# 192 bytes a partition set aside between a kernel's split weights and its operand tiles

## The chip, the core and the metric

The kernel runs on one core of a Trainium2 chip. A core has five engines that run beside each other: PE (TensorE, matmuls; its weight loads are listed apart as PEld), DVE (VectorE), ACT (ScalarE), POOL (GpSimd) and SP (SyncE, which here issues DMAs). They share one on-chip memory of 128 partitions; a tile takes so many bytes in each partition, and an address below is the byte within the partition. The metric is the device time of one execution in microseconds (us), lower is better.

## What is computed

Two layers of a decoder trunk over 256 tokens and 1,024 features, all in float32. Each layer is a mixer and a feed-forward part (FFN), both with adaptive modulation (`w_ada`). Cut to the matrix products that matter here:

```
h    = rms_norm(x) * (1 + sc1) + sh1
proj = h @ w_in[l]                       # 1024 x 10840: q, k, v, index, z, xbc, dt, gates
o_attn = dsa_attention(q, k, v, iq, ik, iw) @ w_attn_o[l]
o_ssm  = gated_norm(ssd_scan(conv(xbc), dt), z) @ w_ssm_o[l]
x    = x + g1 * ((sigmoid(ga) * o_attn + sigmoid(gm) * o_ssm) @ w_out[l])
h    = rms_norm(x) * (1 + sc2) + sh2
val, gate = split(causal_dwconv(h @ w_up[l]))      # 1024 x 5632
x    = x + g2 * ((silu(gate) * val) @ w_down[l])   # 2816 x 1024
```

## The kernel before

**The products.** A float32 product is made of three matmuls of type `float32r`. Each operand is split into a high and a low part, and high x high, high x low and low x high are added up in PSUM. In one matmul one operand is *stationary* (loaded into PE's array first, 128 x 128; this is the PEld row of the profile) and the other is *moving* (streamed past it, 256 or 512 columns). The weights arrive in units of at most 4 x 128 rows by 512 columns (1 MB): `load` (L755) issues the DMA into a tile `st`, and `split_now` (L776) makes `wh` on ACT (a copy with rounding) and `wl = st - wh` on DVE, three buffers each. Activations are split in the same way into pairs of 256 columns.

**Two shapes.** `run_fm` (L798) keeps the weights stationary and moves the activations, 256 columns a matmul; per row block `k` and output block `m` it does

```
mm(o, u["hi"][:, k, ms], ah, kk == 0 and first[m], False)
mm(o, u["hi"][:, k, ms], al, False, False)
mm(o, u["lo"][:, k, ms], ah, False, last)
```

`run_tm` (L847, for q, k, v and the index) does it the other way round: the activations are stationary and 512 columns of the weights move. The trace names a matmul by its operands, the moving one first: `bk<-h,wh` is a moving `h` against a stationary `wh`, `bk<-wh,h` is the `run_tm` form. `bk` is the PSUM bank.

**The moving tiles.** `h` (`h_tile`, L461, pool `hp`, 16 buffers) holds the normalised input of a mixer or an FFN, and later the merged mixer output. `u` (`u_tile`, L456, pool `up`, 39 buffers) holds attention output, scan output and the FFN's activation. The last pairs of an FFN's activation go to `gate` (in the trace `t`, the tag `t2` of pool `wk`) and to `xdt0`/`xdt1`; the last pairs of the scan output go to `xdt` too. The first weight chunk after a norm (`Link`, L546) starts before the norm is known: it uses raw products in tiles `dec` (in the trace `p`, tag `p6` of `wk`) and `cbm`, with 2 columns more, 258 in all.

**Where tiles lie.** A pool's tiles stand one behind the other, in the order in which the pools were opened and the tags first used:

```
cst = ctx.enter_context(tc.tile_pool(name="cst", bufs=1))
wpool = ctx.enter_context(tc.tile_pool(name="wpool", bufs=3))
hp = ctx.enter_context(tc.tile_pool(name="hp", bufs=16))
wk = ctx.enter_context(tc.tile_pool(name="wk", bufs=2))
```

(L441 to L444); `up` is opened later and lies last, up to byte 228,896. `wpool` begins at 26,656, which is 52 x 512 + 32, and all its tiles, those of `hp` and those of `up` are multiples of 512 bytes long. So in the built program every `st`, `wh`, `wl`, `h` and `u` begins at 32 mod 512; so do their slices, which step by 512 bytes (a 128-column block) or 2,048 (a row block). The tiles of `wk` that take part in a product with `wh` and `wl` begin elsewhere because small tiles lie between them:

| moving tile | start mod 512 | minus start of `wh`, `wl` (32), mod 512 |
|---|---|---|
| `h`, `u`, `t` | 32 | 0 |
| `p` | 288 | 256 |
| `xdt`, `cbm` | 480 | 448 |

**What sets the order.** All instructions are recorded and then issued by a planner in the kernel (`commit`, L184; every instruction of the profile therefore has line L201), which fixes each engine's order from its own estimates of cost before anything runs. On the chip each engine works through its queue in that order and waits on semaphores.

**The FFN.** Its first product runs in 11 chunks of 96 matmuls (2 units, 4 output blocks, 4 row blocks each, 3 matmuls); the first chunk is a `Link`. Of each chunk ACT, DVE and POOL make a convolution of width 3 (`conv`, L1857), a tanh gate (`make_ev`, L1867) and the split of the activation (`hi_lo`, L1258), in between the splits of the next weights and the folding of `w_ada` (`adacc`).

Of the kernel before, what the change touches and what calls it, by code (L numbers as in the profile page):

```python
# [10 lines left out]
F32 = mybir.dt.float32  # L11
# [8 lines left out]
P = 128  # L20
# [26 lines left out]
def trunk(ctx, tc, x, c, positions, w_ada, b_ada, norm1_g, w_in, q_norm_g, k_norm_g, ssm_conv_w, ssm_conv_b,  # L47
# [393 lines left out]
    cst = ctx.enter_context(tc.tile_pool(name="cst", bufs=1))  # L441
    wpool = ctx.enter_context(tc.tile_pool(name="wpool", bufs=3))
    hp = ctx.enter_context(tc.tile_pool(name="hp", bufs=16))
    wk = ctx.enter_context(tc.tile_pool(name="wk", bufs=2))  # L444
    pj = ctx.enter_context(tc.tile_pool(name="pj", bufs=4, space=PSUM))
    sm = ctx.enter_context(tc.tile_pool(name="sm", bufs=4, space=PSUM))
# [1481 lines left out]
```

## Time and profile before

| | |
|---|---|
| median of 3 runs | 1256.91 us (1256.19 to 1258.14) |
| the profiled execution | 1256.64 us, of which its span (first to last instruction) is 1254.9 us |
| granted PE clock over the span | 0.998 |
| PE busy | 1229.9 us, 9833 matmuls |
| DVE, ACT, POOL busy | 989.0, 777.3, 478.4 us |
| read from HBM | 243.89 MB, 195 GB/s over the span |

How to read it: the profile is one execution, 0.27 us under the median. Matmuls are pipelined, so the duration of one (about 0.28 us) is latency, and the pace is read from the starts of neighbours. The time goes in this order: to 63 us the opening; 63 to 462 us the mixer of layer 0; 462 to 590 us the first product of its FFN and 590 to about 643 us its `w_down`; then the mixer of layer 1 to 1046 us, its FFN's first product to 1174 us, and `w_down` to the end.

### The profile page before, as it was taken

The page shows a single profiled execution, that of the slowest core. Times are in us where ns is not written, and L with a number is a line of the kernel's source. Part 1 is how long each engine was busy: PE and PEld are TensorE (multiplying, and loading weights), DVE is VectorE, ACT ScalarE, POOL GpSimd, SP SyncE. Part 2 cuts the span into 40 slices and gives each one's busy share as a digit, 9 for nine tenths or more (in the row PEclk, how much of TensorE's full clock was granted, in tenths as well). Part 3 has the DMA queues.
Part 4 walks back from the last instruction along what each step waited for, and adds up shares of the span by engine and source line. Part 5 has one row for each costly group of instructions (what it writes and reads, how often), then busy time and mean ns, then how long its engine had stood idle before and what let it go on. Part 6 is the DMA issues. An engine that isn't in the chain of part 4 may idle for free.

```text
span 1254.9 us, 24795 instructions
## 1 busy us (share of the span) xinstructions
PE 1229.9 (98%) x9833; PEld 1148.5 (92%) x9833; DVE 989.0 (79%) x1549; ACT 777.3 (62%) x1397; POOL 478.4 (38%) x503
## 2 busy tenths in 40 slices
PE   8999999999999999999999999999999999999998
PEld 7777889999999999999996878999999999999998
DVE  5599997877877789998677999887788667887752
ACT  4465767765774477776454476877478435877731
POOL 2162622342343226775121553414316222556500
PEclk9999999999999999999999999999999999999999
DMA  9854654555565747777847555444654665556551
GB/s 296 279 194 144 216 177 143 188 187 185 198 208 191 252 142 252 249 228 243 277 143 270 170 189 177 160 160 160 209 203 162 214 221 177 170 190 197 201 184 52
DMA packets 158665, 246.55 MB, mean 196 GB/s; under 512 B 11868, under 2 KB 66870, under 8 KB 158549
## 3 DMA queue, kind: packets, MB, share of 16 engines
q1 hardware_dynamic: 157989, 244.77, 58.6%
q8 instruction: 77, 1.26, 0.4%
q14 instruction: 39, 0.32, 0.1%
q0 software_dynamic: 288, 0.19, 0.1%
q10 hardware_dynamic: 272, 0.00, 0.0%
HBM read 243.89 MB, written 1.05 MB: 195 GB/s over the span
## 4 chain that ended last, share of the span: by engine, by line
PE 81%; DVE 10%; ACT 3%; POOL 2%; issue 2%; DMA 1%; SPq 0%; DVEq 0%; ACTq 0%; POOLq 0%
PE bk L201 81%; DVE wl L201 3%; POOL w L201 2%; DVE w L201 1%; ACT wh L201 1%; DVE t L201 1%; ACT w L201 1%; DMA ad<-in_w_ada_dram 1%; DVE mx L201 1%; DVE adacc L201 1%; DVE sp_p L201 1%; DVE p L201 1%; POOL rr L201 0%; DVE u L201 0%; DMA rows<-in_b_ada_dram 0%
## 5 line engine op out<-in xcount | busy, mean ns | idle before, releaser
L201 PE MATMUL bk<-h,wh 128*128 128x256 f32 x3296 | 611.9, 286 | 1.2 <-ACT h L201 1.1
L201 PEld LDWEIGHTS bk<-h,wh 128*128 128x128 f32 x3296 | 513.9, 192 | 11.2 <-issue 8.0
L201 DVE TENSOR_TENSOR wl<-st,wh 128x2048 fp32r<-128x2048 f32 (+1 forms) x200 | 438.7, 2199 | 90.4 <-ACT wh L201 89.8
L201 PE MATMUL bk<-h,wl 128*128 128x256 f32 x1648 | 466.3, 283 | 0.0
L201 ACT ACTIVATE wh<-st 128x2048 fp32r<-128x2048 f32 (+1 forms) x200 | 352.5, 1768 | 166.9 <-PE bk L201 113.0
L201 POOL TENSOR_TENSOR w<-w,w 128x254 f32<-128x254 f32 (+2 forms) x213 | 258.4, 1226 | 331.0 <-DVE w L201 227.5
L201 PEld LDWEIGHTS bk<-h,wl 128*128 128x128 f32 x1648 | 315.6, 192 | 0.6 <-DVE wl L201 0.2
L201 PE MATMUL bk<-u,wh 128*128 128x256 f32 x1312 | 240.7, 285 | 0.0
L201 PEld LDWEIGHTS bk<-u,wh 128*128 128x128 f32 x1312 | 203.8, 191 | 2.2 <-issue 2.2
L201 PE MATMUL bk<-u,wl 128*128 128x256 f32 x656 | 185.4, 283 | 0.0
L201 ACT ACTIVATE w<-bk,vec 128x256 f32<-128x256 f32 (+2 forms) x256 | 118.6, 518 | 59.1 <-DVE w L201 33.1
L201 PE MATMUL bk<-wh,h 128*128 128x512 f32 x448 | 145.2, 401 | 3.0 <-ACT wh L201 1.9
L201 PEld LDWEIGHTS bk<-u,wl 128*128 128x128 f32 x656 | 125.5, 191 | 0.0
L201 DVE SCALAR_TENSOR_TENSOR adacc<-ad,chalf,adacc 128x512 f32<-128x512 f32 x140 | 119.2, 852 | 3.1 <-DMA ad<-in_w_ada_dram 2.3
L201 PEld LDWEIGHTS bk<-wh,h 128*128 128x128 f32 x448 | 82.0, 188 | 23.5 <-issue 3.5
L201 DVE SCALAR_TENSOR_TENSOR w<-bk,vec,w 128x255 f32<-128x255 f32 (+1 forms) x176 | 80.0, 476 | 21.3 <-ACT w L201 19.1
L201 PE MATMUL bk<-wl,h 128*128 128x512 f32 x224 | 88.2, 394 | 3.0 <-DVE wl L201 3.0
L201 POOL TENSOR_TENSOR u<-u,u 128x256 f32<-128x256 f32 (+1 forms) x56 | 60.2, 1094 | 59.6 <-DVE u L201 31.7
L201 POOL TENSOR_TENSOR rr<-ss,mhalf 128x16 f32<-128x16 f32 x8 | 33.6, 4195 | 75.3 <-DVE ss L201 75.2
L201 ACT ACTIVATE u<-bk 128x128 f32<-128x128 f32 (+2 forms) x128 | 32.4, 328 | 37.3 <-PE bk L201 37.1
L201 PEld LDWEIGHTS bk<-wl,h 128*128 128x128 f32 x224 | 42.1, 188 | 13.1 <-DVE wl L201 4.5
L201 POOL TENSOR_SCALAR p<-p,sums 128x128 f32<-128x128 f32 x64 | 36.5, 588 | 31.7 <-DVE sums L201 31.7
(225 smaller groups left out, 1383.3 us busy)
## 6 DMA issues: line engine op xcount, KB each, us to landing
st<-in_w_in_dram SPq DMA_DIRECT2D x80, 1024.0 KB, 5.1
st<-in_w_up_dram SPq DMA_DIRECT2D x88, 512.0 KB, 4.5
ad<-in_w_ada_dram SPq DMA_DIRECT2D x160, 256.0 KB, 5.4
st<-in_w_down_dram SPq DMA_DIRECT2D x20, 1024.0 KB, 6.0
st<-in_w_ssm_o_dram SPq DMA_DIRECT2D x16, 1024.0 KB, 5.0
st<-in_w_ada_dram SPq DMA_DIRECT2D x16, 512.0 KB, 9.1
st<-in_w_attn_o_dram SPq DMA_DIRECT2D x8, 1024.0 KB, 5.0
st<-in_w_out_dram SPq DMA_DIRECT2D x8, 1024.0 KB, 5.0
```

The lines of the kernel that those rows point to most:

```text
L201: begun[n].issue()
```

## The change

One tile is asked for in pool `hp` before any `h`, and never written or read:

```diff
@@ -441,6 +441,7 @@
     cst = ctx.enter_context(tc.tile_pool(name="cst", bufs=1))
     wpool = ctx.enter_context(tc.tile_pool(name="wpool", bufs=3))
     hp = ctx.enter_context(tc.tile_pool(name="hp", bufs=16))
+    hp.tile([P, 48], F32, tag="between", name="between", bufs=1)
     wk = ctx.enter_context(tc.tile_pool(name="wk", bufs=2))
     pj = ctx.enter_context(tc.tile_pool(name="pj", bufs=4, space=PSUM))
     sm = ctx.enter_context(tc.tile_pool(name="sm", bufs=4, space=PSUM))
```

48 float32 are 192 bytes. Everything in `hp`, `wk` and `up` moves up by 192; `cst` and `wpool` stay. No instruction is added, removed or moved: row by row each engine's order and its waits are those of before but for the numbers in the buffers' names. The addresses mod 512 become:

| moving tile | start mod 512 | minus start of `wh`, `wl` (32), mod 512 |
|---|---|---|
| `h`, `u`, `t` | 224 | 192 |
| `p` | 480 | 448 |
| `xdt`, `cbm` | 160 | 128 |

In the `run_tm` form the moving `wh`, `wl` stay at 32 and the stationary `h` goes to 224, a difference of 320. Products of two tiles that both lie behind the 192 bytes (`p` with `xdt`, `u` with `u`) keep their difference.

## Rows read from the trace of the kernel before

**Rows 1.** The page's part 1: engine, busy us, share of the span, instructions.

```profile
PE 1229.9 (98%) x9833; PEld 1148.5 (92%) x9833; DVE 989.0 (79%) x1549; ACT 777.3 (62%) x1397; POOL 478.4 (38%) x503
```

**Rows 2.** The page's part 4: chain that ended last, share of the span by engine.

```profile
PE 81%; DVE 10%; ACT 3%; POOL 2%; issue 2%; DMA 1%; SPq 0%; DVEq 0%; ACTq 0%; POOLq 0%
```

**Rows 3.** Stretches: busy us (instructions) of PE, PEld, DVE, ACT, POOL; clock, DMA share, GB/s.

```profile
63.00:168.00 105.00, 101.13 (x616) 83.06 (x614) 98.00 (x201) 67.46 (x146) 51.83 (x42) 1.00 0.53 175
...
462.00:590.00 128.00, 128.00 (x1082) 126.54 (x1082) 118.23 (x143) 97.68 (x161) 84.71 (x65) 1.00 0.73 236
...
663.00:781.00 118.00, 112.65 (x657) 90.24 (x656) 105.17 (x213) 66.47 (x141) 50.42 (x41) 1.00 0.63 214
```

**Rows 4.** Groups of PE's matmuls by shape, whole span: count, busy us, mean ns.

```profile
L201 PE MATMUL bk<-h,wh 128*128 128x256 f32 x3296 | 611.9, 286 | 1.2 <-ACT h L201 1.1
L201 PE MATMUL bk<-h,wl 128*128 128x256 f32 x1648 | 466.3, 283 | 0.0
L201 PE MATMUL bk<-u,wh 128*128 128x256 f32 x1312 | 240.7, 285 | 0.0
L201 PE MATMUL bk<-u,wl 128*128 128x256 f32 x656 | 185.4, 283 | 0.0
L201 PE MATMUL bk<-wh,h 128*128 128x512 f32 x448 | 145.2, 401 | 3.0 <-ACT wh L201 1.9
```

**Rows 5.** PE's timeline at the end of layer 0's `w_down`: start us, us, instruction, count.

```profile
606.44 0.40 PE L201 MATMUL bk<-u,wh 128*128 128x256 f32 x2
...
607.16 0.40 PE L201 MATMUL bk<-t,wh 128*128 128x256 f32 x2
...
607.52 0.40 PE L201 MATMUL bk<-xdt,wh 128*128 128x256 f32 x2
...
607.88 0.39 PE L201 MATMUL bk<-xdt,wh 128*128 128x256 f32 x2
...
610.14 0.28 PE L201 MATMUL bk<-xdt,wl 128*128 128x256 f32 x1
610.25 0.39 PE L201 MATMUL bk<-u,wh 128*128 128x256 f32 x2
```

**Rows 6.** PE's timeline in two `Link` chunks, 258 columns a matmul.

```profile
452.58 0.40 PE L201 MATMUL bk<-p,wh 128*128 128x258 f32 x2
...
455.10 0.40 PE L201 MATMUL bk<-cbm,wh 128*128 128x258 f32 x2
...
653.77 0.41 PE L201 MATMUL bk<-p,wh 128*128 128x258 f32 x2
...
654.51 0.40 PE L201 MATMUL bk<-cbm,wh 128*128 128x258 f32 x2
```

**Rows 7.** PE's timeline in a chunk of the `run_tm` form.

```profile
85.62 0.62 PE L201 MATMUL bk<-wh,h 128*128 128x512 f32 x2
...
87.00 0.27 PE L201 MATMUL bk<-ident,ikr 128*128 128x128 f32 x1
```

**Rows 8.** Groups of PE's matmuls from 63 to 168 us, then from 663 to 781.

```profile
L201 PE MATMUL bk<-h,wh 128*128 128x256 f32 x136 | 26.1, 291 | 0.0
...
L201 PE MATMUL bk<-h,wh 128*128 128x256 f32 x96 | 18.5, 291 | 0.0
```

**Rows 9.** ACT's waits from 168 to 462 us: us in total, times, longest us.

```profile
ACT wh L201 <- PE bk L201: 32.3, 14, 3.8
```

**Rows 10.** Pieces of the chain that ended last, in order of time: start us, us, what.

```profile
394.68 267.64 PE bk L201 x2237
...
1038.13 74.55 PE bk L201 x623
...
1126.37 1.33 DVE wl L201
...
1133.43 3.61 POOL w L201 x2
...
1137.86 1.33 DVE wl L201
```

## The prediction

> **What bounds the kernel now.** I began with the busy shares: PE is busy 98% of the span [rows 1]. Since pipelined matmuls look busy anyway, I then asked the chain of waits, followed back from the last instruction, which puts 81% of the span on PE and 10% on DVE [rows 2]. The stretches show where the rest lies: in the first parts of the two mixers, 63 to 168 us and 663 to 781 us, DVE is busy 98.0 of 105 us and 105.2 of 118 us [rows 3], and there a faster PE gains little. Elsewhere the chain is long pieces of PE alone, such as 267.64 us with 2237 matmuls from 394.68 us on [rows 10]: 0.1196 us a matmul, one behind the other. [...] What counts, then, is the pace of one matmul after the next.
>
> That pace I read from starts. From 606.44 to 607.52 us stand nine matmuls (six with a moving `u`, three with `t`), 1.08 us: 0.120 us each. Then, in the same chunk, against the same kind of stationary tile and with the same 256 columns, come 24 with a moving `xdt`. The first three still take 0.12; from 607.88 to 610.25 us the other 21 take 2.37 us: 0.113 us each [rows 5]. [...] What differs is where the moving tile begins: `u` and `t` lie at the same place mod 512 as `wh` and `wl`, `xdt` 448 further (or 64 before). The trace of before thus holds the experiment that the change makes on most matmuls, at one other distance.
>
> **The change, part by part.** It adds no instruction and moves none in any queue; the 192 bytes cost nothing by themselves, as nothing touches them. What can change is the pace of PE's matmuls, by the distance of their two operands.
>
> *256 columns, `h` and `u` against `wh` and `wl`: distance 0 becomes 192.* There are 3296 + 1648 + 1312 + 656 = 6912 [rows 4]. No row shows distance 192. The nearest rows with these shapes are `xdt` at 448, 0.113 us, and those at 0, 0.120 us; these are the two ends, a gain of 6.7 ns each or nothing. (6.7 is what I take for 0.120 minus 0.113; the rows, given to 0.01 us, allow 6.5 to 7.) I take the gain: 192 and 448 differ by 256, so if the memory repeats in 256 bytes or any smaller power of two the two are the same distance, and if it repeats in 512 both are away from 0, the distance at which the loss is seen in thousands of matmuls.
>
> How many of them lie on the path? In the two DVE stretches are 136 and 96 of `h` against `wh` [rows 8], with the `wl` ones, half as many, 348; I count nothing for them. Each FFN's first product has 10 chunks of 96 after its `Link` chunk, 1920 in both; they are taken apart below. There remain 6912 - 348 - 1920 = 4644, in the later mixer and in `w_down`. There the engines behind PE have room: ACT waits 32.3 us of 168 to 462 us until PE gives back a `wh` buffer [rows 9], so the splits can follow a faster PE. 4644 x 6.7 ns = 31.1 us. I take off a tenth, for matmuls that follow a transpose or an attention product rather than one of their own kind: **28 us**.
>
> *The FFNs.* A chunk is 96 x 0.120 = 11.52 us for PE and would be 96 x 0.113 = 10.85. But in the second FFN the chain leaves PE: the piece of 74.55 us from 1038.13 us is followed by a ring of DVE `wl`, POOL `w` and ACT steps that comes round from the `wl` at 1126.37 to that at 1137.86 us [rows 10], 11.49 us, hardly less than PE's own 11.52. Two of POOL's steps there take 3.61 us. A faster PE runs into this ring: `wl` and the freed banks are late next. In the first FFN DVE is busy 118.2 of 128 us [rows 3], and at PE's new pace 11 chunks would leave it about 121. The bounds are 0 and 960 x 6.7 ns = 6.4 us for each FFN; I take 2 us each, the splits' present lead over PE being used up once: **4 us**.
>
> *512 columns (`wh`, `wl` moving, `h` stationary): distance 0 becomes 320.* [...] No row shows another distance; the nearest is again the 6.7 ns of 256 columns. There are 448 + 224 = 672, nearly all in the opening and the two DVE stretches [rows 3, 4], so of 4.5 us at most I take **1 us**.
>
> *`Link` chunks (258 columns) and `xdt`.* `p` goes from 256 to 448, `cbm` from 448 to 128. At 452.58 to 455.10 us 21 of `p` take 0.120 each; at 653.77 to 654.51 us six of `p` take 0.74 us, 0.123 each [rows 6]. `cbm`, though at 448, is no faster than `p` in its best stretch. I take 0, within 3.3 ns x 288, 1 us, either way. The 192 of `xdt` go to 128 and may lose their 6.7 ns: **-1.3 us**.
>
> **Sum.** 28 + 4 + 1 - 1.3 = 31.7 us off the profiled execution's 1256.6 us: 1224.9. That execution is 0.3 us under the median of 1256.9, so I give **1225 us**.
>
> [...] No row here shows 256 columns under 113.
>
> **The rivals.**
>
> *Other engines take more of it back.* The kernel's order was fixed for the old pace, and wherever a ring as in the second FFN stands hidden under PE, PE now waits for it. If half of the 31.7 us goes, the time is 1241; if three quarters, 1249. For it speaks that DVE is already at 92% in the first FFN; against it that ACT waits for PE in the mixer. What PE waits for would then be `wl` and `w`.
>
> *No change: 192 is no better than 0.* Then it is not the distance that makes `xdt` fast. `cbm` speaks for this: at the same 448 with 258 columns it is not fast at all [rows 6]. Against it speaks that `t` and `xdt`, side by side in one chunk, differ in nothing but their place. Time: 1257, give or take 1.3 for `xdt`. [...]
>
> *Slower: at 192 the two streams meet later and more often.* A weight load reads 512 bytes of each partition, the moving operand 1,024, so a stream that starts 192 ahead can still run into the other within the same matmul. The price has a row: `p` at 256 takes up to 0.123 where the best is 0.120 [rows 6], 3.3 ns. If 192 behaves so, 3.3 ns x 6912 on top, 22.8 us: 1279; with a whole step of 6.7 ns, 1303. It decides from the point where the pace of `h` in the mixers is over 0.120. Against it: 21 of `p` in a row run at 0.120, no worse than distance 0.
>
> **How the numbers follow.** My forecast (most of the gain, 1209 to 1241) gets 0.74; the heavy give-back, 1241 to 1254, 0.07; no change 0.11; slower 0.08. The low end: all 6912 and the 512-column ones gaining on the path would be 46.3 + 4.5 = 51 us, 1206; since the DVE stretches and the FFNs exclude most of that, 1209 it is. The high end must reach into the give-back case to hold 8 in 10: 1250. A measurement of this kernel tells about 0.2%, 2.5 us, from no change, so faster is 0.74 + 0.07 = 0.81, same 0.11, slower 0.08.
>
> **What would show it.** If right: starts of `h` and `u` matmuls 0.113 us apart in the mixers and in `w_down`; PE's waits for DVE and ACT grown by several us, above all in the FFNs; chunks of the second FFN still near 11.5 us; the DVE stretches as long as now; `xdt` perhaps back at 0.120. If starts stay 0.120 apart, the step on the distance is wrong; if they are 0.113 apart and the time hardly falls, the step on the other engines is.

## The result and the profile after

The changed kernel takes 1244.33 us (median of 4 runs, 1240.05 to 1246.18) where the kernel before takes 1256.78 (4 runs, 1256.19 to 1258.14). The ratio is 0.9895, with a 95% interval of 0.9867 to 0.9922: **12.5 us faster**. That lies inside the predicted range of 1209 to 1250, but it is about two fifths of the 31.7 us that the prediction added up.

The profiled execution of after is its fastest, 1240.05 us with a span of 1238.3 us, 16.6 us less than the span of before. So two gaps need an explanation: 31.7 us forecast against 16.6 us between the profiles, and 16.6 against 12.5 between the medians.

First the page of after, its busy shares and the chain that ended last, to set beside [rows 1, 2]:

```profile
PE 1206.7 (97%) x9833; PEld 1122.9 (91%) x9833; DVE 991.0 (80%) x1549; ACT 776.7 (63%) x1397; POOL 475.5 (38%) x503
...
PE 77%; DVE 12%; ACT 5%; POOL 3%; issue 3%; DMA 0%; DVEq 0%; ACTq 0%; POOLq 0%
```

PE is busy 23.2 us less with as many matmuls, and the other engines do what they did. In the chain PE falls from 81 to 77% and DVE and ACT gain two points each. PE got faster, and some of that turned into waiting. The groups of PE's matmuls, after [rows 4]:

```profile
L201 PE MATMUL bk<-h,wh 128*128 128x256 f32 x3296 | 591.5, 282 | 1.2 <-ACT h L201 1.1
...
L201 PE MATMUL bk<-h,wl 128*128 128x256 f32 x1648 | 459.5, 279 | 1.2 <-DVE wl L201 1.2
...
L201 PE MATMUL bk<-u,wh 128*128 128x256 f32 x1312 | 233.4, 281 | 0.0
...
L201 PE MATMUL bk<-wh,h 128*128 128x512 f32 x448 | 146.6, 404 | 3.1 <-ACT wh L201 2.0
```

The groups with 256 columns lost 20.4, 6.8 and 7.3 us of busy time. The one with 512 columns gained 1.4. How the 256-column matmuls got faster is read from starts, as in [rows 5], at the same place in the program (PE's timeline of after: start, us, instruction, count):

```profile
596.36 0.28 PE L201 MATMUL bk<-u,wl 128*128 128x256 f32 x1
...
597.42 0.29 PE L201 MATMUL bk<-t,wl 128*128 128x256 f32 x1
597.54 0.27 PE L201 MATMUL bk<-ident,adarow 128*128 128x128 f32 x1
...
598.01 0.39 PE L201 MATMUL bk<-u,wh 128*128 128x256 f32 x2
...
599.03 0.40 PE L201 MATMUL bk<-xdt,wh 128*128 128x256 f32 x2
599.27 0.28 PE L201 MATMUL bk<-xdt,wl 128*128 128x256 f32 x1
...
601.76 0.28 PE L201 MATMUL bk<-xdt,wl 128*128 128x256 f32 x1
```

Nine matmuls from 596.36 to 597.42 us take 1.06 us, 0.1178 each. Then comes one matmul of another kind (`ident,adarow`), and behind it nine from 598.01 to 599.03 take 1.02 us, **0.1133** each. Tiles, shapes and distance are the same in both. Seven triples of `xdt` (now at 128) take 2.49 us, 0.1186 each. I took the starts of all 2,090 triples of `h` and `u` in which `wh`, `wh`, `wl` follow one another. Before, 82% of them take 357 to 364 ns. After, none does: 52% take 336 to 343 ns (0.1133 us a matmul) and 40% take 350 to 356 (0.1178). Nearly all of the rest take over 400 ns. Of two neighbouring triples with nothing between them, both run at the fast pace in 1,000 cases and both at the slow one in 728; 47 pairs go from slow to fast and none from fast to slow. So at distance 192 there are two paces, both faster than the old one, and a run at the fast one keeps it until a matmul of another kind interrupts.

PE's waits in the two kernels (us in total, times, longest), before and then after:

```profile
PE bk L201 <- DVE wl L201: 3.0, 4, 1.6
```

```profile
PE bk L201 <- DVE wl L201: 4.1, 8, 1.6
PE bk L201 <- ACT adarow L201: 3.2, 1, 3.2
...
PE bk L201 <- DVE adacc L201: 2.2, 1, 2.2
```

Before, the wait for `adarow` was 0.4 us and none was put down to `adacc`. Both belong to the `w_ada` modulation, which is folded beside the FFNs. The stretches of after, beside [rows 3]:

```profile
63.00:168.00 105.00, 100.17 (x615) 82.02 (x614) 97.98 (x203) 67.59 (x146) 51.61 (x42) 1.00 0.52 173
462.00:590.00 128.00, 125.79 (x1093) 124.28 (x1092) 117.93 (x141) 94.01 (x155) 82.56 (x63) 0.99 0.75 241
...
663.00:781.00 118.00, 112.93 (x665) 90.25 (x666) 108.93 (x225) 71.75 (x154) 50.43 (x43) 0.99 0.56 189
```

In the first FFN PE is no longer busy for all 128.00 us but for 125.79. In the second the chain now leaves PE at 1060.43 us, where before a piece of PE held it to 1112.68 [rows 10]. Behind that it runs over DVE, ACT and POOL, and comes to the ring of [rows 10] (chain of after, in order of time):

```profile
1024.52 35.91 PE bk L201 x302
...
1108.09 3.60 POOL w L201 x2
1112.51 1.33 DVE wl L201
...
1119.58 3.61 POOL w L201 x2
1124.00 1.33 DVE wl L201
```

1124.00 minus 1112.51 is 11.49 us, the ring's period before. Its `wl` stands on the chain five times, the last at 1158.50, as often as before.

Matched matmul by matmul (PE's order is the same in both), the difference of the two profiles splits like this, with each part's share of the forecast. A matmul is counted from its start to the start of the next one, so a wait stands in the row of the matmul behind which it comes:

| part | forecast gain, us | pace | waits behind | net |
|---|---|---|---|---|
| 256 columns in the later mixers and `w_down` | 28 | 17.7 | -2.7 | 15.0 |
| 256 columns in the FFNs | 4 | 8.4 | -3.8 | 4.6 |
| 256 columns in the two DVE stretches | 0 | 1.1 | -0.5 | 0.6 |
| 512 columns | 1 | -1.7 | 0.9 | -0.8 |
| `Link` and `xdt` | -1.3 | -1.0 | 0.0 | -1.0 |
| other matmuls | 0 | -0.9 | -1.0 | -1.9 |
| sum | 31.7 | | | 16.5 |

Of the first row, 4644 matmuls gained 3.8 ns each, not 6.7. Its wait is that for `adarow`, 3.16 us against 0.42. In the second row the first FFN lost about 2.4 us to the wait for `adacc`, the second about 1.4 to three waits for `wl`.

**From 16.6 to 12.5.** The clock rows suggest what the medians add. PE's timeline of after around its wait for `adacc`:

```profile
530.81 0.28 PE L201 MATMUL bk<-h,wl 128*128 128x256 f32 x1
533.30 0.59 PE L201 MATMUL bk<-adacc,ones 128*32 128x128 f32 x8 [2.21 <-DVE adacc L201]
...
534.62 0.63 PE L201 MATMUL bk<-h,wh 128*128 128x256 f32 x2
...
535.26 0.63 PE L201 MATMUL bk<-h,wh 128*128 128x256 f32 x2
```

and the stretch behind it (columns as in [rows 3]):

```profile
533.50:536.70 3.20, 3.20 (x22) 2.89 (x14) 3.20 (x4) 2.37 (x6) 2.77 (x2) 0.50 0.91 288
```

After 2.21 us of idling the granted clock is 0.50, and a triple takes 0.64 us instead of 0.34. The profile of before has one such stretch inside the run, that of after two, 3.4 us each. The other three runs of after have a mean clock of 0.994 against 0.997 in the profiled one; 0.003 of 1240 us is 3.7 us, as an estimate, and their spans are 3.3 to 6.2 us longer. Of these three only the mean clock is kept, so that they lost it behind a wait is inferred. The runs of before scatter by 2 us, those of after by 6.

### The profile page after: what moved, and what is told of

Read it like the earlier page. It is cut to its first block, busy times and chain, and to the rows that moved or that the text cites. A ratio compares the mean times of both kernels' runs of the same rounds, so it can differ in the third digit from the quotient of the medians.

```text
span 1238.3 us, 24795 instructions
## 1 busy us (share of the span) xinstructions
PE 1206.7 (97%) x9833; PEld 1122.9 (91%) x9833; DVE 991.0 (80%) x1549; ACT 776.7 (63%) x1397; POOL 475.5 (38%) x503
## 4 chain that ended last, share of the span: by engine, by line
PE 77%; DVE 12%; ACT 5%; POOL 3%; issue 3%; DMA 0%; DVEq 0%; ACTq 0%; POOLq 0%
PE bk L201 77%; DVE wl L201 5%; DVE w L201 3%; POOL w L201 2%; ACT wh L201 2%; ACT w L201 2%; DVE adacc L201 1%; DVE t L201 1%; DVE u L201 1%; POOL rr L201 0%; DVE mx L201 0%; ACT u L201 0%; DVE p L201 0%; POOL rows L201 0%; DVE sp_p L201 0%
## 5 line engine op out<-in xcount | busy, mean ns | idle before, releaser
L201 PE MATMUL bk<-h,wh 128*128 128x256 f32 x3296 | 591.5, 282 | 1.2 <-ACT h L201 1.1
L201 PEld LDWEIGHTS bk<-h,wh 128*128 128x128 f32 x3296 | 502.1, 189 | 11.4 <-issue 8.6
L201 PE MATMUL bk<-h,wl 128*128 128x256 f32 x1648 | 459.5, 279 | 1.2 <-DVE wl L201 1.2
L201 POOL TENSOR_TENSOR w<-w,w 128x254 f32<-128x254 f32 (+2 forms) x213 | 253.8, 1205 | 322.4 <-DVE w L201 223.7
L201 PEld LDWEIGHTS bk<-h,wl 128*128 128x128 f32 x1648 | 310.8, 189 | 2.8 <-DVE wl L201 2.4
L201 PE MATMUL bk<-u,wh 128*128 128x256 f32 x1312 | 233.4, 281 | 0.0
L201 PEld LDWEIGHTS bk<-u,wh 128*128 128x128 f32 x1312 | 199.4, 189 | 2.2 <-issue 2.2
L201 PE MATMUL bk<-u,wl 128*128 128x256 f32 x656 | 182.9, 279 | 0.0
```

Source lines behind the costliest of these rows:

```text
L201: begun[n].issue()
```

## The experiments

The theories carry letters, in the order in which they came up. Each expectation says what its theories give for its run.

### The pace by distance, PE alone

A kernel with nothing but the triples of `run_fm` and `run_tm` on two resident pairs of tiles, every distance in steps of 32 bytes. It leaves the whole computation out.

```diff
+    for j in range(16):
+        fm(f"fd{LETTERS[j]}", 32 * j)      # 256 columns, moving operand 32*j bytes ahead
+    fm("shiftg", 192, at=192)              # both operands moved by 192, distance 192
+    for j in (0, 6, 8, 14):
+        fm(f"ld{LETTERS[j]}", 32 * j, units=2, n=S + 2)
+    for j in range(16):
+        tm(f"td{LETTERS[j]}", 32 * j)      # 512 columns of the weights moving
```

> Leaves out the whole computation (the output is a copy of x): PE alone runs the triple of matmuls of the weight chunks from one stationary and one moving buffer, 144 matmuls of 256 columns at each of 16 distances mod 512 between moving and stationary start (0, 32 to 480), four distances again in another order, two with both operands moved by 192, four with 258 columns, and 16 of the form with 512 moving columns. Theory A, the distance sets the pace by the meeting of the two reads: 0.120 us at 0 and at 0 with both moved, 0.113 at 448, two paces (0.113 and 0.118) or one of them at 192, 0.117 to 0.120 at 128; the same at each distance when it comes again. Theory B, only the place of the moving operand counts: both moved by 192 is as fast as distance 192. Theory C, the second pace at 192 (0.118) comes from other engines that use the memory: with these engines idle 192 is at 0.113 throughout. 512 columns: 0.227 at 0 and, by the profile of the changed kernel, 0.229 to 0.232 at 320.

Groups of PE's matmuls by shape (count, busy us, mean ns; `fdi` is distance 256, `againa` 0, `fdg` 192, `fdo` 448; `tda` and `tdg` are the 512-column form at 0 and 192):

```profile
L36 PE MATMUL fdi<-mv,wt 128*128 128x256 f32 x144 | 17.4, 283 | 0.0
...
L36 PE MATMUL againa<-mv,wt 128*128 128x256 f32 x144 | 17.4, 283 | 0.0
...
L36 PE MATMUL fdg<-mv,wt 128*128 128x256 f32 x144 | 16.5, 276 | 0.0
...
L36 PE MATMUL fdo<-mv,wt 128*128 128x256 f32 x144 | 16.5, 276 | 0.0
...
L36 PE MATMUL tdg<-wt,mv 128*128 128x512 f32 x48 | 11.2, 392 | 0.0
...
L36 PE MATMUL tda<-wt,mv 128*128 128x512 f32 x48 | 11.1, 390 | 0.0
```

By starts, in us a matmul: 0.1200 at 0, 0.1178 at 32 and 64, 0.1200 at 96, 0.1187 at 128, 0.1173 at 160, **0.1133 at 192**, 0.1183 at 224, and the same eight again from 256 on. Both operands moved by 192 give 0.1200 at distance 0 and 0.1133 at 192, so it is the distance that counts and not the place, and it repeats in 256 bytes. With 512 columns 0 is the best distance, 0.2267; 192 (the stationary operand ahead, as in the change) gives 0.2289, the others 0.232 to 0.234. With 258 columns it is 0.1200 at 0 and 256, and 0.1219 at 192 and 448. Of the theories in the text B falls. C seemed to hold, since here all of 192 runs at 0.1133. The next run showed why that was too early.

### What comes before a run of matmuls

PE alone again, runs of 48 matmuls at one distance with something else in between (thirteen distances, ten runs at each).

```diff
+    BREAKS = (("full", 1), ("full", 2), ("full", 3), ("short", 1), ("short", 2), ("short", 3), ("wide", 1), ("wide", 2), ("wide", 3))
...
+        fm(name, d, units=1)
+        for kind in BREAKS:
+            between(kind)
+            fm(name, d, units=1)
```

> Leaves out the whole computation (the output is a copy of x). PE alone: at each of 13 distances mod 512 (0, 64, 128, 160, 176, 184, 188, 192, 196, 200, 208, 224, 448) the run of 48 matmuls of 256 columns comes ten times, with another kind of matmul between: 1 to 3 of 128 float32 columns, 1 to 3 of 16 columns, 1 to 3 of 512 columns. Theory D, the slower pace at 192 (0.118) is a second steady state of PE alone that the entry picks: some of the ten runs at 192 and at 448 stand at 0.118 to their end, the others at 0.113; at 0 all are at 0.120, at 64 all at 0.118. Theory C, the slower pace comes from other engines' accesses: all ten at 192 are at 0.113. Open: whether a distance near 192 (184, 188, 196, 200) has the 0.113 alone.

PE's timeline, distance 192 (`dh`):

```profile
462.97 5.70 PE L35 MATMUL dh<-mv,wt 128*128 128x256 f32 x48
468.51 0.60 PE L35 MATMUL break<-ones 128*128 128x128 f32 x4
468.87 5.90 PE L35 MATMUL dh<-mv,wt 128*128 128x256 f32 x48
...
487.18 5.69 PE L35 MATMUL dh<-mv,wt 128*128 128x256 f32 x48
```

The same 48 matmuls take 5.70 us behind one break and 5.90 behind another. The last 24 of each run are 113.3 or 117.8 ns apart and nothing else, five of the ten each way, in the same sequence at 192 and at 448. At distance 0 all are at 120.0. No other engine works here. So **D** holds, and C falls: at 192 PE itself has two steady paces, and what it did just before picks one. This is the 40% of slower triples in the kernel. One forecast missed: at 64, where all ten were to be at 0.118, two are at 113.3 ns. Of the distances near 192 none has the fast pace: 188 has 117.8 and 118.9, 196 has 121.7.

### 256 bytes instead of 192

```diff
-    hp.tile([P, 48], F32, tag="between", name="between", bufs=1)
+    hp.tile([P, 64], F32, tag="between", name="between", bufs=1)
```

> 256 bytes in the place of 192, so that h and u stand at distance 256. Theory A with the repeat of 256 bytes that the sweep showed: the pace is 0.120 as at 0 and the time that of before, 1257, within 2. Theory A with a repeat of 512 bytes, as the change's words have it: both reads begin at different places and the time falls to 1245 or lower.

1258.5 us against 1258.48, ratio 0.9997 (0.9987 to 1.0006): nothing. `h` and the weights now begin at different places mod 512, and it does not help; 82% of the triples take 357 to 364 ns as before. What counts is the distance mod 256.

### 448 bytes instead of 192

```diff
-    hp.tile([P, 48], F32, tag="between", name="between", bufs=1)
+    hp.tile([P, 112], F32, tag="between", name="between", bufs=1)
```

> 448 bytes in the place of 192: distance 448, the one that xdt had in the kernel before. With a repeat of 256 bytes the same as the change: both paces (0.113 and 0.118) mixed, 1241 to 1247. If 448 is better than 192 (the 21 xdt matmuls in a row at 0.113): all at 0.113 and 1230 to 1236.

1242.7 us, ratio 0.9884 (0.9866 to 0.9902), the same as the change. 43% of the triples are at 0.1133 and 49% at 0.1178, and the same waits appear. Its profiled run is the longest of its four, 1247.31 us, and shows what scatters. PE's timeline at the wait for `adarow`, and the stretch behind it:

```profile
1166.93 0.48 PE L201 MATMUL bk<-ident,adarow 128*128 128x128 f32 x1 [3.24 <-ACT adarow L201]
```

```profile
1166.10:1172.70 6.60, 5.77 (x27) 5.77 (x28) 4.63 (x6) 3.53 (x7) 4.94 (x5) 0.50 0.43 158
```

and the same wait in after:

```profile
1163.14 0.33 PE L201 MATMUL bk<-ident,adarow 128*128 128x128 f32 x1 [3.15 <-ACT adarow L201]
```

```profile
1150.00:1175.00 25.00, 21.84 (x195) 21.32 (x195) 19.64 (x26) 18.39 (x32) 15.20 (x15) 1.00 0.56 184
```

The wait of 3.24 us ends at 1166.93. From shortly before its end PE's granted clock is 0.50, 6.6 us in this stretch, some 5.8 us of it behind the wait; in the other run, with 3.15 us of idling at the same place, it stays at 1.00. So the wait at the end of the FFN costs its own 3.2 us, and in this run about 3 us more, as an estimate: half of the 5.8.

### A planner that reckons with the new pace

The planner's cost of a matmul goes from 118.5 to 115.5 ns (256 columns) and from 227.5 to 230 (512).

```diff
-            return ns + 9.5 + 0.4258 * max(n, S)
+            return ns + (230.0 if n > S + 2 else 115.5)
```

> The change, and the planner reckons 115.5 ns for a matmul of 256 columns and 230 for one of 512 (118.5 and 227.5 before), near what the changed kernel's trace shows; this moves instructions. If part of the gain is lost because the order was fixed for the old pace (PE's waits of 7 us in all for wl, adacc and adarow in the profile of the change): 1238 to 1241. If those waits are there whatever the planner reckons: 1243 to 1246.

1245.18 us, ratio 0.9892 (0.9875 to 0.9908): no gain over the change. The new order has one long wait of its own:

```profile
639.45 0.66 PE L201 MATMUL bk<-adacc,ones 128*32 128x128 f32 x8 [9.62 <-DVE adacc L201]
```

and 10.24 us at half clock, from 634.36 to 644.60 us: they begin within the wait, and 5.2 us of them lie behind it. Counted by matmuls started, this kernel was 1.5 us ahead of the change at 590 us and 10.5 us behind it at 643.

### Folds held back, with and without the 192 bytes

Theory E holds that PE, faster than the order was made for, waits for the folds of `w_ada`. Its remedy, on top of the edit before: the planner is told that PE's use of a fold has 4 or 8 us to spare.

```diff
-            by = now[0] + AHEAD
+            by = now[0] + AHEAD - self.spare
...
-        hot.append(later(Need(row, banks=1), rest()))
+        hot.append(later(Need(row, banks=1, spare=4000.0), rest()))
...
-                yield Need(acc, banks=1)
+                yield Need(acc, banks=1, spare=8000.0)
```

> The run before (planner reckons 115.5 and 230 ns) and the planner also lets the folding of w_ada onto PE only when its inputs are 8 us (the sum adacc) and 4 us (the row adarow) older than it asked before. In that run PE waits 9.9 us for adacc, nearly all in one wait of 9.6 us, with 10.2 us of half clock behind it. Theory E, a third of the lost gain is that PE, faster than the order was made for, waits for these folds: no such wait is left and the time is 1230 to 1236. If these waits only stood in front of others (the ring of DVE, POOL and ACT in the FFNs): 1242 to 1246.

1255.52 us, ratio 0.9983 (0.9973 to 0.9994): 11 us worse than the change. The waits grew instead of going away (14.8 us for `adacc` against 9.9), so the remedy failed; why they grew is open. But the order can be used for something else: run it without the 192 bytes.

```diff
-    hp.tile([P, 48], F32, tag="between", name="between", bufs=1)
```

> The same order without the 192 bytes: what the new order is worth by itself. Theory E: nothing or little, 1254 to 1259, since PE at 0.120 hardly waited for the folds. If the new order is better whatever the pace: as far under 1258 as e6_spare is under the change.

1280.41 us, ratio 1.0180 (1.0164 to 1.0196). PE's waits with the 192 bytes, and then without:

```profile
PE bk L201 <- DVE adacc L201: 14.8, 2, 10.6
PE bk L201 <- DVE wl L201: 6.1, 5, 2.9
```

```profile
PE bk L201 <- DVE adacc L201: 14.8, 2, 10.6
PE bk L201 <- DVE wl L201: 7.2, 6, 3.0
```

In this pair, with the same order on every engine, the 192 bytes bring 24.9 us from median to median, and 25.1 us between the profiles. The 256-column matmuls give 26.4, the waits behind them 0.0. That is nearly the pace gain of the change (27.2 in the table). Here nearly all of it becomes time, since PE's waits are as long with as without. In the order of the kernel before, 7.0 us of it are paid back as new waits.

### Where the low parts lie

PE alone: 64 settings, the moving operand at 32 i bytes and the low part of the weights at 32 j, five entries each.

```diff
-                    wh, wl = weights(0, k, m * P, P, at), weights(1, k, m * P, P, at)
+                    wh, wl = weights(0, k, m * P, P, at), weights(1, k, m * P, P, at + low)
```

> Leaves out the whole computation (the output is a copy of x). PE alone, 64 settings, each entered five times with another matmul between: the moving tiles stand 0 to 224 bytes (in steps of 32) after the high part of the weights, and the low part 0 to 224 bytes after the high part. Is there a setting with 0.113 at all five entries? If the second steady state belongs to distance 192 as such: none, the best mean near 115.5 ns at 192 with the low part at 0. If the three matmuls of a triple hold each other in the slower state only while they stand alike: some setting with the low part moved stays at 113.3 from every entry, and the kernel would gain up to 2 ns on each of 6912 matmuls, 14 us, by it.

One setting has 113.3 ns at all five entries: moving 192, low part 128 (`mge`). With the low part at 0, as in the change (`mga`), four of five are at 113.3 and one at 117.8. The others are mostly between 117 and 120 ns. By groups (240 matmuls each; `maa` is 0 and 0):

```profile
L35 PE MATMUL maa<-mv,wt 128*128 128x256 f32 x240 | 30.9, 288 | 0.0
...
L35 PE MATMUL mga<-mv,wt 128*128 128x256 f32 x240 | 28.5, 278 | 0.0
L35 PE MATMUL mge<-mv,wt 128*128 128x256 f32 x240 | 28.3, 277 | 0.0
```

### The low parts moved too

`wl` gets 128 bytes of its own, and the piece in `hp` shrinks so that `h` and `u` stay at 192; every engine's order is that of the kernel before.

```diff
-    hp.tile([P, 48], F32, tag="between", name="between", bufs=1)
+    hp.tile([P, 16], F32, tag="between", name="between", bufs=1)
...
+        if "below" not in pools:
+            pools["below"] = wpool.tile([P, 32], F32, tag="below", name="below", bufs=1)
```

> The change, with the low parts of the weights (wl) also moved, by 128 bytes a partition, so that h and u stand 192 ahead of wh and 64 ahead of wl mod 512; every engine's order is that of the kernel before. In the sweep of 64 settings (192, 128) was the only one with 0.1133 us a matmul at all five entries. Theory D (PE alone has two steady paces at a distance of 192, and the entry picks one) with that sweep: nearly all triples take 340 ns, next to none 353.5; the matmuls of 256 columns save 38 to 46 us instead of 27.3, PE's new waits for the other engines grow from 7 to 15 or 20, and the time is 1228 to 1240 us. If instead the second pace is made by the other engines' traffic, the low parts' place changes nothing: about 40% of the triples stay at 353.5 and the time at 1242 to 1247.

**1233.6 us**, ratio 0.9815 (0.9796 to 0.9835): 24.3 us faster than before, and its interval lies wholly below that of the change. PE's timeline at the place shown above:

```profile
592.78 0.39 PE L201 MATMUL bk<-u,wh 128*128 128x256 f32 x2
...
593.46 0.27 PE L201 MATMUL bk<-ident,adarow 128*128 128x128 f32 x1
...
593.92 0.39 PE L201 MATMUL bk<-u,wh 128*128 128x256 f32 x2
...
594.94 0.40 PE L201 MATMUL bk<-xdt,wh 128*128 128x256 f32 x2
```

The six matmuls before `ident,adarow` take 0.68 us and the nine behind it 1.02: 0.1133 each on both sides. Over the kernel 83% of the triples are at 0.1133 and 3% at 0.1178 (5% at 0.120). The 256-column matmuls give 34.6 us and the waits behind them take 8.7, where I had reckoned 15 or 20. Theory D is thus shown in the kernel. The second pace is not made by the other engines' traffic, which is unchanged. My bounds of 38 to 46 us for the pace were too high: the triples at 336 to 343 ns, four fifths of all, gain 35.7 us, and the rest, mostly next to an interruption, gain nothing.

### The same with the planner at 117.5 and 115.0 ns

```diff
-            return ns + 9.5 + 0.4258 * max(n, S)
+            return ns + 8.5 + 0.4258 * max(n, S)
```

and with 6.0 in the place of 8.5.

> The run before with a planner that reckons 117.5 ns for a matmul of 256 columns instead of 118.5, so that the order of the other engines follows a faster PE a little. If what is lost to waits comes from an order made for the old pace, PE's waits shrink and the time is 2 to 6 us below that of the run before it; if each order has its own accidental wait (as with 115.5, where one wait for adacc took 9.6 us), it is the same or up to 12 us worse.

> As the run before it with 115.0 ns. The first theory: 4 to 10 us below the run with the old planner. The second: the same or up to 15 us above it, with one or two waits of PE for adacc of over 5 us in the rows, and a stretch at half clock behind each.

With 117.5 it takes 1235.52 us, ratio 0.9817 (0.9802 to 0.9831), no different. With 115.0 it takes 1237.95, ratio 0.9844 (0.9827 to 0.9860), if anything worse, and its rows show the accidental wait:

```profile
PE bk L201 <- DVE adacc L201: 9.3, 4, 5.5
```

It comes with 10.24 us at half clock, from 629.69 us, which begin within the wait.

In three tries (115.5 with the change, 117.5 and 115.0 here) reckoning with the true pace brought nothing. The waits are not a matter of one constant. Whether an order exists that hides them was not found out.

## Why the prediction was right and wrong

**Right.** The operands' distance sets the pace, and the trace of before held the evidence, the fast `xdt` in [rows 5]. No change and slower both fell. Why the pace goes by the distance, and why there are two paces at 192, no run shows; that two reads meet, as theory A and the slower rival have it, was my guess. With PE alone the same matmuls take 0.1133, 0.1178 or 0.1200 us with nothing changed but bytes of distance or what ran before. The FFNs were right in kind, with a ring still at 11.49 us, but their size is in part luck: 4 us forecast and 4.6 measured, of which 8.4 is pace and 3.8 waits, and over half of the waits is for the fold `adacc`, which I had not named. `xdt` lost what 128 costs (0.1186 us a matmul, 0.113 before), and the DVE stretches stayed as long as they were.

**Wrong, and the main miss: the term 4644 x 6.7 ns.** The count was right, the price was not: it measured 3.8 ns. I read 6.7 ns from 21 matmuls in a row behind one entry, and took it for the price of a distance. It is the better of two steady paces: 0.1133 in 52% of the triples and 0.1178 in 40%. With what matmuls near an interruption miss, that comes to 17.7 us for 31.1. Among the triples of this term the slow pace is even the commoner, 692 against 636; at 4.5 ns a matmul these miss, as an estimate, 9.3 of the 13.4 us. The tenth that I took off for interruptions covers 3.1. The step that failed is the one from one run of rows to all of them. Looking back, the trace of before has four such runs of `xdt`, two in each `w_down`, and in all four the triples settle at 340 ns or next to it. The second steady pace is not in it. What it does show, and what I did not weigh, is that the short groups of `xdt` in the mixers begin with a triple of 353 ns before one of 341: the gain depends on what ran before.

**Not counted: the last `w_down`'s wait.** The later mixers paid back nothing, as forecast. But the last `w_down`, which I had counted with them, pays 2.7 us for `adarow`. I had named `wl` and the freed banks as late next; the folds of `w_ada` were late first, with 2.2 and 3.2 us in one wait each.

**Wrong in sign: 512 columns.** I let them gain by the nearest row, that of 256 columns. Alone they run at 0.2267 at distance 0 and 0.2289 at 192, and in the kernel their pace lost 1.7 us.

**The argument on the repeat** needed only 256 bytes or less, and 256 is what the runs show. But "if it repeats in 512 both are away from 0" was no safeguard: away from 0 lie 0.1133, 0.1173 and 0.1200, depending on the distance.

**The slower rival's price** was misread: `p`'s 0.123 at 653.77 us is not due to distance 256, where 258 columns alone run at 0.1200. And `cbm`, my witness for no change, was none: with 258 columns the distances 192 and 448 cost 0.1219.

**Not in the sum at all:** with the longer waits come, in some runs, 3.4 to 6.8 us at half clock. By the mean clocks that is most of the 4.3 us by which the median of after is longer than the profiled run. The give-back rival (1241 to 1249) gives the right time, and the measured one lies in the band to which I gave 0.07, but mostly by another cause: of the 15.1 us between the forecast and the profiles the first row of the table holds 13.0, and 10.3 of that is pace.

## What to carry to other kernels

Where matmuls follow one another closely, look at where the moving and the stationary operand begin, mod 256 bytes: a few bytes set aside were worth 2 to 5.6% of PE's pace here, and 1 to 2% of the kernel's time. Measure the distances for your own shape and sequence (here 192, with the low parts at 128) over several entries, since one fast run of rows may be one of two states. And when an engine gets faster in a kernel whose order was fixed for the old pace, price the waits of every stage that hands a result on, and the clock behind each of them, before you count the gain.

## What was not expected of the hardware

- Two steady paces of the same instructions, 113.3 and 117.8 ns, picked by what PE did before. At 64 too, two of ten entries ran at 113.3 and eight at 117.8.
- A few bytes decide: 120.0 ns at 184 and 200, 113.3 or 117.8 at 192, and 121.7 at 196, slower than distance 0. As an estimate, 196 would have cost 1.7 ns x 6912, 12 us.
- The best pace of 256 columns in any setting was 113.3 ns, and that of 512 columns 226.7.
- Through a wait of 3.15 us PE's granted clock stayed at 1.00 in one run; in another it fell to 0.50 before the end of a wait of 3.24 us at the same place.
